# Two token tiles first: reordering attention's output projection, with two plain units instead of three in the FFN behind it

## The chip, the cores and the metric

The kernel runs on one core of a Trainium2 chip. The metric is device time in microseconds, here the median of several executions. Engines are named as in the profile: PE (matmuls), PEld (PE's weight loads), DVE (vector engine), ACT (scalar engine), POOL and SP (which here mostly issue transfers).

## The reference

A trunk of two layers over 512 tokens of width 1024, all in float32. Layer 0 mixes tokens by stick-breaking attention with 16 heads, layer 1 by a gated token MLP; each is followed by a SwiGLU FFN of width 2816. The part that matters is attention's output projection, the residual step, and the first FFN:

```python
y = o.transpose(0, 2, 1, 3).reshape(B, S, D) @ w_o          # attention's projection
x = x + gate * rms_norm(y, mix_post_g[i])
shift, scale, gate = ada_modulation(c, ffn_ada_w[i], ffn_ada_b[i])
h = rms_norm(x, ffn_pre_g[i]) * (1.0 + scale) + shift
y = (jax.nn.silu(h @ w_gate) * (h @ w_up)) @ w_down
x = x + gate * rms_norm(y, ffn_post_g[i])
```

## The kernel before, in words

**Numbers in two parts.** Every matmul operand is split into a rounded high part and a low part (`split`, line 128), and every product is three matmuls, high by high, high by low and low by high (`mm3`, line 120). ACT writes the high part and DVE the low part. Weights are loaded raw into two buffers (`wraw`) and split into a pair of tiles `wh` and `wl`. These come from `wpool` with five slots, to which `wpool2` with one is added after attention; `wtile` (line 184) takes them in turn from the pools that exist when it is called. A slot is free again when the last matmul that reads it is done.

**The stream of weights.** `stream` is one list of all weights in the order of use. `wget(key, look)` hands out the next one and splits those up to `look` places ahead (3 unless said otherwise) where that hasn't been done.

**Attention and filler.** Eight head pairs are worked on in an order written out by hand. Between their steps a generator, `filler`, puts in other matmuls, a group of three at a time: first the q and k of later pairs (112 groups), then the beginning of the output projection for token tiles 3 and 2 (16 groups: `NEARLY` = 4 of the 8 weight slabs, two tiles, two halves of 512 columns). `FIRST`, `FILLS` and `LAST` say how many groups go into each place.

**The projection (`out_proj`).** There are four tiles of 128 tokens, each with two PSUM banks, which is all eight banks. The first slabs go through all tiles (tiles 2 and 3 have slabs 0 to 3 already); the last `J` = 4 slabs are kept and applied tile by tile in the order 0, 1, 2, 3, so that the tiles finish one after another. After each comes `boundary`: squares on ACT, scaling, the residual sum and the second norm on DVE, a store of x by POOL's queue, eight transposes on PE, and the split of the transposed result (`hTh`, `hTl`). Tiles 0 and 1 are the lower 256 tokens, tiles 2 and 3 the upper. From attention's end on, the order within an engine is the scheduler's, which goes by program order and by what is ready, within the dependencies (several matmuls into one bank keep their order).

**The first FFN.** Its 2816 hidden columns are 22 units of 128. A plain unit (`Ffn.unit`) multiplies gate and up separately, and can do 256 tokens alone. A seven-product unit (`seven`) makes both by seven products of sums of weights with sums of the transposed halves, S1 to S4. Its weights are built by `blocks` from `rawx` and `rawy` (three `wh`/`wl` pairs and one smaller). The sums combine a lower tile with its upper one: `boundary` keeps a copy `c` of the lower tiles, and `sums` makes S1 to S4 when the upper ones are there. Now there are three plain units (`NH` = 3) and 19 seven-product units. The lower halves of the three plain units run among the boundaries of tiles 2 and 3, the upper halves after them, then the seven-product units begin. The weights that `wget` emits in the second of them stand in the program inside the last boundary (`mid`).

The FFN's products are in this order, each over four k:

```python
product(R1, "A11", "B11", True, False)
product(R2, "A12", "B21", True, True)
product(R3, "1", "T1", True, False)
product(R1, "2", "T2", False, False)
product(R3, "4", "B22", False, True)
product(R1, "3", "T3", False, False)
product(R1, "A22", "T4", False, True)   # in rest(), inside the next unit
```

Of the kernel before, what the change touches and what calls it, by code (L numbers as in the profile page):

```python
# [33 lines left out]
def trunk(ctx: ExitStack, tc: tile.TileContext, A: dict, out: bass.AP):  # L34
# [273 lines left out]
        ap = A[key]  # L308
        stream.append((ap[idx], a, b, (key,) + idx))

    NH = 3
    wadd("wv", 2, 512, 0, 0)
    wadd("wqk", 8, P, 0, 0)
    wadd("wqk", 8, P, 0, 1)
# [7 lines left out]
    for k in range(KD):  # L322
        wadd("wo", 1, D, k)
    for l in range(2):
        for f in range(NH):
            wadd("wgu", 8, P, l, f, 0)
            wadd("wgu", 8, P, l, f, 1)
        for f in range(NH, KF):
            stream.append((None, 0, 0, ("blocks", (l, f - NH))))
        if l == 1:  # L330
            for q in range(2):
                for p in PAIRS[q]:
                    wadd("wdn", 4, 256, q, p)
        if l == 0:
            for f in range(KF):
                wadd("wdown", 1, D, f)
            for j in range(4):
# [152 lines left out]
        lo %= 256  # L490
        return h[:, k % 4, lo : lo + n], l[:, k % 4, lo : lo + n]

    def boundary(s, tt, y, xin, hT, S, tag, mid=None):
# [12 lines left out]
        xd[tt] = dram.tile([P, D], F32, tag=f"x{tt}", bufs=2, name=nm("xd"))  # L506
        nc.gpsimd.dma_start(out=xd[tt][:], in_=x)
        sx = small.tile([P, 1], F32, tag="sx", name=nm("sx"))
        feature[1] = act.activation(junk[:], x[:], AF.Square, accum_out=sx[:])
        sd, r1 = rms(sx[:])  # L510
        dve.tensor_tensor(t[:], x[:], ada["A", s], ALU.mult)
        dve.reciprocal(r1[:], sd[:])
        feature[0] = dve.scalar_tensor_tensor(
            t[:], t[:], r1[:, 0:1], ada["B", s], ALU.mult, ALU.add
        )
        late = []
        if mid is not None:
            mid()
            chain = pe["prev"]
        for q in range(2):  # L520
            ps = bank("tp", tag)
            for k in range(4):
                kk = q * 4 + k
                transpose(ps[:, k * P : (k + 1) * P], t[:, kk * P : (kk + 1) * P])
                if mid is not None and kk == 0:
                    order(last_tp[0], chain)
            a = ps[:].rearrange("p (a b) -> p a b", a=4)
            if tt % 2 == 0:
                hT[tt // 2, q] = (slot(F32R, "hTh", 4, 256), slot(F32R, "hTl", 4, 256))
            c = slice(tt % 2 * P, (tt % 2 + 1) * P)  # L530
            th, tl = hT[tt // 2, q]
            split(th[:, :, c], tl[:, :, c], a)
            if S is not None and tt < 2:
                if tt == 0:
                    S["c", q] = slot(F32, "c", 4, 256)
                act.activation(S["c", q][:, :, tt * P : (tt + 1) * P], a, AF.Copy)
            late.append(a)
        return lambda: sums(S, tt, late)

    def sums(S, tt, a):  # L540

# [27 lines left out]
        return t  # L569


    def out_proj(s, nk, get_act, wkey, J, bg, hT, nxt=(), pre=None, S=None, steps=0, bg2=None):

# [6 lines left out]

        def step(k, tt, a, w, halves=(0, 1)):
            for hf in halves:
                if k == 0 or k == mid and tt == last:
                    y[tt][hf] = bank("y", "p" if tt == last else "b")
                mm3(
                    y[tt][hf][:],
                    a[0][:, tt * P : (tt + 1) * P], a[1][:, tt * P : (tt + 1) * P],
                    w[0][:, 0, hf * 512 : (hf + 1) * 512],  # L590
                    w[1][:, 0, hf * 512 : (hf + 1) * 512],
                    k == 0 or k == mid and tt == last, k == nk - 1 or k + 1 == mid and tt == last,
                )

        npre = 0
        if pre is not None:
            npre = len(pre["w"])
            for tt in pre["y"]:
                y[tt] = pre["y"][tt]
        for k in range(nk - J):  # L600
            a = get_act(k)
            w = pre["w"][k] if k < npre else wget(wkey(k))
            for tt in range(NT):
                if k >= npre or tt not in pre["y"]:
                    step(k, tt, a, w)
# [10 lines left out]
            (k, get_act(k), wget(wkey(k), J + 1 if k == nk - J else 0))  # L616
            for k in range(nk - J, nk)
        ]
        sqrt_table()
        xs = {tt: x_load(tt) for tt in range(2)}  # L620
        xin = xs.get
        for tt in range(NT):
            for hf in range(2):
                for k, a, w in tail:
                    step(k, tt, a, w, (hf,))
            if tt == last and yp is not None:
                for hf in range(2):
                    dve.tensor_tensor(yp[:, hf, :], y[tt][hf][:], yp[:, hf, :], ALU.add)
                y[tt] = [yp[:, hf, :] for hf in range(2)]
            if tt < 2:  # L630
                boundary(s, tt, y[tt], xin, hT, S, "p" if last == 0 else "b")
                xs[tt + 2] = x_load(tt + 2)
        evacs, late = [], []
        for n, tt in enumerate((2, 3)):
# [5 lines left out]
            if nxt and tt == 2:  # L640
                evacs.append(nxt[0]())
            late.append(
                boundary(
                    s, tt, y[tt], xin, hT, S, "p" if tt == 3 else "b",
                    mid if nxt and tt == 3 else None,
                )
            )
        if nxt:
            evacs.append(nxt[2]())
            with tc.issue_after(last_sqrt[0].ins):  # L650
                for f in evacs:
                    f()
# [204 lines left out]
    with tc.tile_pool(name="att", bufs=1) as att, tc.tile_pool(name="att2", bufs=2) as att2:  # L857
# [282 lines left out]
    fwork["pool"] = fpool  # L1140

    class Ffn:
        def __init__(self, s, li, hT, S):
            self.s, self.li, self.hT, self.S = s, li, hT, S
            self.act = []
            self.ws = {}

        def w(self, f, look):
            if f not in self.ws:
# [22 lines left out]
            return evac  # L1172

        def first(self):
            return [lambda f=f: self.unit(f, 0, 256, 2) for f in range(NH)]

        def seven(self, f, pending, bg0):

            W = wget(("blocks", (self.li, f - NH)), 0)
# [52 lines left out]
            return rest  # L1232

        def units(self, bg0):
            for f in range(NH):
                self.unit(f, 256, 256)()
            rest = None
            for f in range(NH, KF):
                if f == NH:
                    act.chain = True  # L1240
                if f == NH + 1:
# [215 lines left out]
    def gmlp(bg, hT, nhT, nS, nxt):  # L1457
# [120 lines left out]
def _layout(i):  # L1578
# [31 lines left out]
    a["wx"], a["wy"] = [np.stack(t) for t in zip(*[blocks(g[3:], u[3:]) for g, u in gu])]  # L1610
# [66 lines left out]
```

## Time and profile before

| | |
|---|---|
| device time, median of 3 runs | 1106.31 us (1104.22 to 1106.82) |
| span of the profiled execution | 1104.6 us, 18512 instructions |
| PE busy | 1085.9 us (98%) |
| DVE busy | 945.9 us (86%) |
| ACT busy | 594.2 us (54%) |
| first matmul of the projection outside attention | about 243.4 us |
| first seven-product unit of the first FFN begins | 312.5 us |

No time of the profiled execution is given besides its span, from its first to its last instruction; the span lies between the lowest and the highest of the three times. A busy PE is not a PE at its peak, because matmuls overlap: a matmul of 512 columns is shown with some 390 ns, while one starts every 227 ns. So the cost of matmuls is read from the chain of waits, where a stretch of them is given with its length and count. In the rows, `y` is the projection's output, `tp` the transposes, `gu` a plain unit's gate and up, `r` the banks of a seven-product unit, `raw` a loaded weight, `fs` and `Sl` the sums.

### The profile page before, as it was taken

What the parts mean: (1) busy time and instruction counts of PE and PEld (TensorE: products, weight loads), DVE (VectorE), ACT (ScalarE), POOL (GpSimd) and SP (SyncE); (2) the same over time, 40 slices, a digit from 0 to 9 for tenths busy, and PEclk for the clock granted to TensorE, in tenths of its full rate; (3) what the DMA queues carried; (4) which work ended last, traced back from release to release, by engine and by line L of the source; (5) the groups of instructions that cost most, each with busy time, mean ns of one, the idle gap of its engine ahead of it and who ended that gap; (6) DMA issues with size and microseconds to landing.
All of it is one profiled execution on the core that took longest, in us unless ns stands there. A gap on an engine that the chain in (4) does not pass through costs nothing.

```text
span 1104.6 us, 18512 instructions
## 1 busy us (share of the span) xinstructions
PE 1085.9 (98%) x7404; PEld 979.0 (89%) x7404; DVE 945.9 (86%) x1248; ACT 594.2 (54%) x982; POOL 29.5 (3%) x53
## 2 busy tenths in 40 slices
PE   6999999999999999999999999999999999999997
PEld 4787788788999999998888889988999999989996
DVE  4988999966989999989866967668979999899997
ACT  6554665665655555554243626426555555565662
POOL 0020100000000000000000000001000000000000
PEclk9999999999999999999999999999999999999999
DMA  8976434304433434359757465334334343333252
GB/s 302 370 226 217 142 116 133 125 11 152 157 112 131 162 119 146 132 197 351 272 191 256 144 205 196 96 116 155 128 117 155 128 159 102 110 115 96 77 187 81
DMA packets 51355, 176.38 MB, mean 160 GB/s; under 512 B 6074, under 2 KB 9146, under 8 KB 51268
## 3 DMA queue, kind: packets, MB, share of 16 engines
q1 hardware_dynamic: 48708, 166.81, 44.6%
q0 software_dynamic: 2560, 8.39, 2.1%
q8 instruction: 58, 0.95, 0.3%
q14 instruction: 29, 0.24, 0.1%
HBM read 164.69 MB, written 8.39 MB: 157 GB/s over the span
## 4 chain that ended last, share of the span: by engine, by line
PE 90%; DVE 4%; DMA 2%; ACT 2%; issue 1%; SPq 0%; DVEq 0%; ACTq 0%
PE r L109 32%; PE y L109 18%; PE pqk L109 7%; PE gu L109 6%; PE v L109 5%; PE X L109 4%; PE u L109 4%; PE Y L109 3%; PE av L109 2%; PE z L109 2%; PE tw L117 1%; PE tp L117 1%; PE Z L109 1%; PE W L109 1%; PE ab L109 1%
## 5 line engine op out<-in xcount | busy, mean ns | idle before, releaser
L87 ACT ACTIVATE wh<-raw 128x1024 fp32r<-128x1024 f32 (+1 forms) x112 | 115.7, 1038 | 130.5 <-PE y L109 39.4
L109 PE MATMUL r<-Sh,wh 128*128 128x256 f32 x608 | 168.1, 276 | 0.5 <-ACT e L87 0.5
L109 PE MATMUL r<-Sh,wl 128*128 128x256 f32 x608 | 167.9, 276 | 0.0
L109 PE MATMUL r<-Sl,wh 128*128 128x256 f32 x608 | 167.9, 276 | 0.0
L109 PE MATMUL y<-wh,as 128*128 128x512 f32 x480 | 149.9, 390 | 0.0
L178 DVE TENSOR_TENSOR wl<-raw,wh 128x1024 fp32r<-128x1024 f32 x87 | 105.8, 1222 | 48.2 <-ACT wh L87 47.6
L109 PEld LDWEIGHTS r<-Sh,wh 128*128 128x128 f32 x608 | 114.1, 188 | 1.0 <-ACT e L87 0.9
L109 PEld LDWEIGHTS r<-Sl,wh 128*128 128x128 f32 x608 | 114.1, 188 | 0.1
L109 PEld LDWEIGHTS r<-Sh,wl 128*128 128x128 f32 x608 | 114.1, 188 | 0.0
L109 PEld LDWEIGHTS y<-wh,as 128*128 128x128 f32 x480 | 90.0, 188 | 18.6
L71 DVE TENSOR_TENSOR wl<-f,wh 128x1024 fp32r<-128x1024 f32 x87 | 103.2, 1220 | 0.0
L87 ACT ACTIVATE wh<-f 128x1024 fp32r<-128x1024 f32 x87 | 91.8, 1055 | 15.3 <-DVE f L71 11.6
L87 ACT ACTIVATE e<-r 128x256 f32<-128x256 f32 x114 | 43.7, 385 | 101.8 <-PE r L109 100.8
L109 PE MATMUL y<-wl,as 128*128 128x512 f32 x240 | 93.7, 391 | 0.0
L109 PE MATMUL r<-hTh,wh 128*128 128x256 f32 x304 | 84.2, 277 | 0.2 <-DVE gu L71 0.2
L109 PE MATMUL r<-hTl,wh 128*128 128x256 f32 x304 | 84.0, 276 | 0.0
L109 PE MATMUL r<-hTh,wl 128*128 128x256 f32 x304 | 84.0, 276 | 0.0
L109 PE MATMUL r<-hTh,b 128*128 128x256 f32 x304 | 57.9, 276 | 0.0
L109 PEld LDWEIGHTS r<-hTh,wh 128*128 128x128 f32 x304 | 57.1, 188 | 0.9 <-DVE gu L71 0.9
L109 PEld LDWEIGHTS r<-hTh,wl 128*128 128x128 f32 x304 | 57.1, 188 | 0.0
L109 PEld LDWEIGHTS r<-hTl,wh 128*128 128x128 f32 x304 | 57.1, 188 | 0.0
L87 ACT ACTIVATE wh<-rawx 128x1024 fp32r<-128x1024 f32 x38 | 40.4, 1063 | 29.8 <-PE r L109 29.0
(262 smaller groups left out, 2937.1 us busy)
## 6 DMA issues: line engine op xcount, KB each, us to landing
rawada<-in_ada SPq DMA_DIRECT2D x80, 512.0 KB, 5.7
rawy<-in_wy SPq DMA_DIRECT2D x38, 512.0 KB, 4.6
rawx<-in_wx SPq DMA_DIRECT2D x38, 512.0 KB, 3.7
raw<-in_wdown SPq DMA_DIRECT2D x22, 512.0 KB, 5.4
raw<-in_wdn SPq DMA_DIRECT2D x22, 512.0 KB, 3.6
raw<-in_wqk SPq DMA_DIRECT2D x16, 512.0 KB, 3.9
ada<-in_ada0p SPq DMA_DIRECT2D x12, 512.0 KB, 6.3
raw<-in_wgu SPq DMA_DIRECT2D x12, 512.0 KB, 3.5
```

Source lines behind the costliest of these rows:

```text
L71: b = getattr(nc.vector, op)(*args, **kw)
L87: b = nc.scalar.activation(*args, **kw)
L109: b = nc.tensor.matmul(o, l, r, start=start, stop=stop, skip_group_check=True)
L117: last_tp[0] = nc.tensor.transpose(o, i, ident)
L178: last_low[0] = nc.vector.tensor_tensor(l[:], raw[:], h[:].bitcast(F32), ALU.subtract)
```

## The change

1. `NH` is 2 for the first FFN and 3 for the second. The first FFN has two plain units and 20 seven-product units. The arrays `wx` and `wy` hold one block more.
2. `NEARLY` is 5: slab 4 of the projection is applied to tiles 3 and 2 in attention too, so the filler has 20 groups there. `LAST` has four groups more, one in head pair 6 and three in head pair 7.
3. With `up=True`, slabs 0 to 3 are not applied to tiles 0 and 1 at the projection's beginning. Those tiles start with slab 4. `J` is 2. The tiles finish in the order 2, 3, 0, 1; tiles 0 and 1 take slabs 6 and 7 and then slabs 0 to 3 (`early`).
4. `boundary` keeps the copy `c` of the upper tiles, and `sums_up` makes S1 at once from their two halves; S2, S4 and S3 follow after tiles 0 and 1.
5. The plain units do the upper 256 tokens first, among the boundaries of tiles 0 and 1, and the lower ones after.

```diff
-    NH = 3
+    NH = 2, 3
...
-        for f in range(NH, KF):
-            stream.append((None, 0, 0, ("blocks", (l, f - NH))))
+        for f in range(NH[l], KF):
+            stream.append((None, 0, 0, ("blocks", (l, f - 2))))
...
-            if S is not None and tt < 2:
-                if tt == 0:
+            if S is not None and tt in lead:
+                if tt % 2 == 0:
                     S["c", q] = slot(F32, "c", 4, 256)
-                act.activation(S["c", q][:, :, tt * P : (tt + 1) * P], a, AF.Copy)
+                act.activation(S["c", q][:, :, c], a, AF.Copy)
             late.append(a)
-        return lambda: sums(S, tt, late)
+        if lead == (0, 1):
+            return lambda: sums(S, tt, late)
+        return lambda: sums_up(S, tt, late)
+
+    def sums_up(S, tt, a):
...
+        if tt > 1:
+            dve.tensor_tensor(f[:, 0], c0, c1, ALU.subtract)
+            part("1", f[:, 0])
+            return
+        g = npool.tile([P, 2, 4, P], F32, tag="n", name=nm("fs"))
+        dve.tensor_tensor(f[:, 0], a[0], c0, ALU.subtract)
+        dve.scalar_tensor_tensor(f[:, 1], f[:, 0], -1.0, c1, ALU.mult, ALU.subtract)
+        part("2", f[:, 1])
+        dve.tensor_tensor(g[:, 1], f[:, 1], a[1], ALU.add)
+        part("4", g[:, 1])
+        part("3", f[:, 0])
...
-        for k in range(nk - J):
+        for k in range(npre - 1 if up else 0, nk - J):
...
+        early = [(k, get_act(k), pre["w"][k]) for k in range(npre - 1)] if up else []
         sqrt_table()
-        xs = {tt: x_load(tt) for tt in range(2)}
+        seq = (2, 3, 0, 1) if up else (0, 1, 2, 3)
+        xs = {tt: x_load(tt) for tt in seq[:2]}
         xin = xs.get
-        for tt in range(NT):
+        for n, tt in enumerate(seq):
             for hf in range(2):
-                for k, a, w in tail:
+                for k, a, w in tail + (early if n > 1 else []):
                     step(k, tt, a, w, (hf,))
...
-            evacs.append(nxt[2]())
+            evacs.extend(f() for f in nxt[2:])
...
-        NEARLY = 4
+        NEARLY = 5
...
-        LAST = (2, 2, 2, 2, 2, 2, 1), (1, 1, 1, 1, 1, 1, 1), (2, 0, 2, 0, 2, 2, 0)
+        LAST = (2, 2, 2, 2, 2, 2, 1), (2, 1, 1, 1, 1, 1, 1), (3, 1, 2, 1, 2, 2, 0)
...
-            return [lambda f=f: self.unit(f, 0, 256, 2) for f in range(NH)]
+            return [lambda f=f: self.unit(f, self.lo, 256, 2) for f in range(self.nh)]
...
-    f0, f1 = Ffn(1, 0, hT1, S1), Ffn(3, 1, hT3, S3)
+    f0, f1 = Ffn(1, 0, hT1, S1, 256), Ffn(3, 1, hT3, S3, 0)
     out_proj(
         0, KD, lambda k: (o8[k][:, 0, :], o8[k][:, 1, :]), lambda k: ("wo", k),
-        4, bg, hT1, f0.first(), early, S1,
+        2, bg, hT1, f0.first(), early, S1, up=True,
     )
```

More of the change, by code (lines that the diff above doesn't have):

```diff
@@ L324, in trunk @@
     for l in range(2):
-        for f in range(NH):
+        for f in range(NH[l]):
             wadd("wgu", 8, P, l, f, 0)
             wadd("wgu", 8, P, l, f, 1)
-        for f in range(NH, KF):
-            stream.append((None, 0, 0, ("blocks", (l, f - NH))))
+        for f in range(NH[l], KF):
+            stream.append((None, 0, 0, ("blocks", (l, f - 2))))
         if l == 1:
@@ L491, in hB, with boundary @@
         return h[:, k % 4, lo : lo + n], l[:, k % 4, lo : lo + n]
-    def boundary(s, tt, y, xin, hT, S, tag, mid=None):
+    def boundary(s, tt, y, xin, hT, S, tag, mid=None, lead=(0, 1)):
         halves = [slice(0, 512), slice(512, D)]
@@ L532, in boundary, with part @@
             split(th[:, :, c], tl[:, :, c], a)
-            if S is not None and tt < 2:
-                if tt == 0:
+            if S is not None and tt in lead:
+                if tt % 2 == 0:
                     S["c", q] = slot(F32, "c", 4, 256)
-                act.activation(S["c", q][:, :, tt * P : (tt + 1) * P], a, AF.Copy)
+                act.activation(S["c", q][:, :, c], a, AF.Copy)
             late.append(a)
-        return lambda: sums(S, tt, late)
+        if lead == (0, 1):
+            return lambda: sums(S, tt, late)
+        return lambda: sums_up(S, tt, late)
+    def sums_up(S, tt, a):
+        c = slice(tt % 2 * P, (tt % 2 + 1) * P)
+        if tt % 2 == 0:
+            for n in "1" if tt == 2 else "324":
+                S[n] = (slot(F32R, "Sh", 4, 256), slot(F32R, "Sl", 4, 256))
+        c0, c1 = [S["c", q][:, :, c] for q in range(2)]
+        f = npool.tile([P, 2, 4, P], F32, tag="n", name=nm("fs"))
+        def part(n, f):
+            split(S[n][0][:, :, c], S[n][1][:, :, c], f)
+        if tt > 1:
[9 more added lines that the diff above has]
+        part("3", f[:, 0])
     def sums(S, tt, a):
@@ L569, in x_load, with out_proj @@
         return t
-    def out_proj(s, nk, get_act, wkey, J, bg, hT, nxt=(), pre=None, S=None, steps=0, bg2=None):
+    def out_proj(s, nk, get_act, wkey, J, bg, hT, nxt=(), pre=None, S=None, steps=0, bg2=None, up=False):
         last = 0 if steps else 3
@@ L584, in step @@
             for hf in halves:
-                if k == 0 or k == mid and tt == last:
+                if k == (npre - 1 if up else 0) or k == mid and tt == last:
                     y[tt][hf] = bank("y", "p" if tt == last else "b")
@@ L591, in step @@
                     w[1][:, 0, hf * 512 : (hf + 1) * 512],
-                    k == 0 or k == mid and tt == last, k == nk - 1 or k + 1 == mid and tt == last,
+                    k == (npre - 1 if up and tt < 2 else 0) or k == mid and tt == last,
+                    k == (npre - 2 if up and tt < 2 else nk - 1) or k + 1 == mid and tt == last,
                 )
@@ L629, in out_proj @@
                 y[tt] = [yp[:, hf, :] for hf in range(2)]
-            if tt < 2:
-                boundary(s, tt, y[tt], xin, hT, S, "p" if last == 0 else "b")
-                xs[tt + 2] = x_load(tt + 2)
+            if n < 2:
+                f = boundary(
+                    s, tt, y[tt], xin, hT, S, "p" if tt == last else "p" if last == 0 else "b",
+                    None, seq[:2],
+                )
+                xs[seq[n + 2]] = x_load(seq[n + 2])
+                if up:
+                    f()
         evacs, late = [], []
-        for n, tt in enumerate((2, 3)):
+        for n, tt in enumerate(seq[2:]):
             def mid():
@@ L638, in mid @@
                 edge[0] = False
-            if nxt and tt == 2:
+            if nxt and n == 0:
                 evacs.append(nxt[0]())
@@ L644, in out_proj @@
                     s, tt, y[tt], xin, hT, S, "p" if tt == 3 else "b",
-                    mid if nxt and tt == 3 else None,
+                    mid if nxt and n == 1 else None, seq[:2],
                 )
@@ L1142, in trunk, with __init__ @@
     class Ffn:
-        def __init__(self, s, li, hT, S):
-            self.s, self.li, self.hT, self.S = s, li, hT, S
+        def __init__(self, s, li, hT, S, lo):
+            self.s, self.li, self.hT, self.S, self.lo = s, li, hT, S, lo
             self.act = []
             self.ws = {}
+            self.nh = NH[li]
         def w(self, f, look):
@@ L1174, in first @@
         def first(self):
-            return [lambda f=f: self.unit(f, 0, 256, 2) for f in range(NH)]
+            return [lambda f=f: self.unit(f, self.lo, 256, 2) for f in range(self.nh)]
         def seven(self, f, pending, bg0):
-            W = wget(("blocks", (self.li, f - NH)), 0)
+            W = wget(("blocks", (self.li, f - 2)), 0)
             prep = ahead()
@@ L1234, in units @@
         def units(self, bg0):
-            for f in range(NH):
-                self.unit(f, 256, 256)()
+            for f in range(self.nh):
+                self.unit(f, 256 - self.lo, 256)()
             rest = None
-            for f in range(NH, KF):
-                if f == NH:
+            for f in range(self.nh, KF):
+                if f == self.nh:
                     act.chain = True
-                if f == NH + 1:
+                if f == self.nh + 1:
                     pe["chain"] = dve.chain = act.chain = True
@@ L1609, in _layout @@
     a["wgu"] = np.stack([np.stack([g[:3], u[:3]], 1) for g, u in gu])
-    a["wx"], a["wy"] = [np.stack(t) for t in zip(*[blocks(g[3:], u[3:]) for g, u in gu])]
+    a["wx"], a["wy"] = [np.stack(t) for t in zip(*[blocks(g[2:], u[2:]) for g, u in gu])]
     a["wdown"] = slabs(i["ffn_w_down"][0])
```

## The prediction, made before the change was run

> **What bounds the kernel now.** I read the page first, then the stretches around the change, the chain of waits, and last the timelines of ACT and DVE in those stretches.
>
> ```profile
> span 1104.6 us, 18512 instructions
> PE 1085.9 (98%) x7404; PEld 979.0 (89%) x7404; DVE 945.9 (86%) x1248; ACT 594.2 (54%) x982; POOL 29.5 (3%) x53
> PE 90%; DVE 4%; DMA 2%; ACT 2%; issue 1%; SPq 0%; DVEq 0%; ACTq 0%
> ```
>
> PE is the bound nearly everywhere, so a change gains only matmuls that vanish or PE idle time that is filled. By stretch (time, then busy time of PE, PEld, DVE, ACT, POOL):
>
> ```profile
> 229.00:243.40 14.40, 13.98 (x88) 11.77 (x85) 7.93 (x11) 7.97 (x13) 0.00 (x0) 1.00 0.01 1
> 243.40:257.70 14.30, 14.30 (x65) 11.83 (x64) 8.18 (x9) 7.34 (x11) 0.00 (x0) 1.00 0.38 111
> 257.70:316.90 59.20, 58.84 (x434) 54.70 (x432) 55.00 (x79) 36.24 (x70) 3.12 (x5) 1.00 0.46 152
> 317.10:494.00 176.90, 176.90 (x1553) 176.72 (x1554) 159.41 (x209) 99.51 (x169) 0.96 (x1) 1.00 0.40 139
> ```
>
> These are the last head pair of attention, the start of its projection, the passage into the first FFN, and that FFN's seven-product units. In the passage PE is full, but DVE is busy 55.0 of 59.2: a second bound close behind. The chain and PE's waits there:
>
> ```profile
> 243.42 22.23 PE y L109 x98
> ...
> 277.46 5.71 PE gu L109 x48
> 283.18 0.87 PE tp L117 x8
> 284.05 5.50 PE gu L109 x48
> 289.55 1.08 PE tp L117 x8
> 290.63 21.88 PE gu L109 x192
> 312.51 4.09 PE r L109 x36
> ...
> 316.65 0.39 ACT e L87
> ...
> 317.09 163.78 PE r L109 x1440
> ...
> PE av L109 <- DVE ar L71: 0.8, 1, 0.8
> PE r L109 <- ACT e L87: 0.5, 1, 0.5
> PE av L109 <- ACT ar L87: 0.4, 1, 0.4
> ```
>
> A projection matmul costs 22.23/98 = 0.227 us, an FFN matmul 163.78/1440 = 0.1137 us. All PE idle that the change could fill is 0.8 + 0.4 + 0.5 = 1.7 us.
>
> **The change, part by part.**
>
> *Two plain units instead of three.* A plain unit has 2 x 2 x 8 x 3 = 96 matmuls, a seven-product unit 7 x 4 x 3 = 84. 12 x 0.1137 = -1.4 us. The extra unit's preparation lies beside PE: in its stretch ACT is busy 99.5 and DVE 159.4 of 176.9. Two weight loads go and two of the same size come.
>
> *Four projection steps moved into the last two head pairs.* 12 matmuls x 0.227 = 2.7 us move; they gain only where PE waits there, so 0 to -1.2. I take -0.4, the last pair's gap, since the added steps stand right ahead of that wait.
>
> *The weight slots.* This decides it. The rounded weights live in five slots of `wpool`; the sixth, `wpool2`, joins only after attention. `wget` rounds three slabs ahead, so with `NEARLY` = 5 all eight projection slabs are assigned to the five. Slabs 0 to 3 are now read by the last matmuls of tiles 0 and 1, so four slots stay taken to the end of the projection, and slabs 4, 5, 6 and 7 pass one after another through the fifth. Within a bank the accumulation keeps its order, so slabs 0 to 3 cannot go first. Rows of ACT (start, duration, what ended its idle time) and one of DVE show what a slot that comes free costs:
>
> ```profile
> 246.19 1.07 ACT L87 ACTIVATE wh<-raw 128x1024 fp32r<-128x1024 f32 x1 [0.28 <-PE y L109]
> 248.91 1.06 ACT L87 ACTIVATE wh<-raw 128x1024 fp32r<-128x1024 f32 x1 [1.65 <-PE y L109]
> 252.27 1.06 ACT L87 ACTIVATE wh<-raw 128x1024 fp32r<-128x1024 f32 x1 [2.30 <-DMA raw<-in_wo]
> ...
> 247.29 1.23 DVE L178 TENSOR_TENSOR wl<-raw,wh 128x1024 fp32r<-128x1024 f32 x1 [0.33 <-ACT wh L87]
> ```
>
> The first two are slabs 5 and 6 waiting for slabs 0 and 1. Today PE has other slabs meanwhile; after the change it has none. It stands from its last matmul to the end of ACT's rounding: 1.07 plus about 0.25 for the matmul's tail and the two signals, 1.3 us. DVE's low part (1.23) is covered by the first product of the eight banks, 8 x 0.227 = 1.8. Three hand-overs: +3.9 us; from 0 (if another slot is found) to 3 x 2.6 = 7.8 (if the low part isn't covered). Slab 7's load is issued when slab 5's rounding frees its raw buffer, some 9 us before it is due, so SP adds nothing. Behind ACT's waiting rounding stand only the squares of tiles not yet finished.
>
> *Reordered tail.* Matmuls and transposes (4 x 8) are the same in number. But slab 7 starts only when all tiles have had slab 6, so tiles 2 and 3 finish together and late. From 243.4: +2.7 - 0.4 of moved work = 245.7; slab 4 for two tiles 2.7; then stall 1.3 and slab 5 5.4, the same for slab 6, and stall 1.3: 263.2. Tile 2 ends some 2 us later and its first multiplication on DVE starts at 265.5. Tile 0's starts now at
>
> ```profile
> 257.79 0.69 DVE L71 TENSOR_TENSOR t<-y,G 128x512 f32<-128x512 f32 x1 [0.70 <-ACT junk L87]
> ...
> 313.45 1.29 DVE L71 TENSOR_TENSOR Sl<-fs,Sh 128x512 fp32r<-128x512 f32 x2
> ...
> 314.98 1.22 DVE L71 TENSOR_TENSOR wl<-f,wh 128x1024 fp32r<-128x1024 f32 x1
> ```
>
> and the passage's DVE work ends at 314.98 + 1.22 = 316.2, the last sum at 314.7. DVE's groups in that stretch (count, then busy and mean ns):
>
> ```profile
> L178 DVE TENSOR_TENSOR wl<-raw,wh 128x1024 fp32r<-128x1024 f32 x5 | 5.9, 1220 | 0.0
> L71 DVE TENSOR_TENSOR hTl<-tp,hTh 128x512 fp32r<-128x512 f32 x8 | 5.3, 686 | 0.4
> L71 DVE TENSOR_TENSOR Sl<-fs,Sh 128x512 fp32r<-128x512 f32 x8 | 5.3, 686 | 0.1
> L71 DVE TENSOR_TENSOR wl<-f,wh 128x1024 fp32r<-128x1024 f32 x4 | 4.9, 1220 | 0.0
> L71 DVE TENSOR_TENSOR f<-rawx,rawy 128x1024 f32<-128x1024 f32 x2 | 2.5, 1225 | 0.6 <-DMA rawx<-in_wx 0.6
> L71 DVE TENSOR_TENSOR wl<-rawx,wh 128x1024 fp32r<-128x1024 f32 x2 | 2.4, 1224 | 0.3 <-ACT wh L87 0.3
> L71 DVE TENSOR_TENSOR act<-silu,gu 128x256 f32<-128x256 f32 x6 | 2.3, 414 | 0.0
> ```
>
> *S1 at the upper boundaries.* Sixteen operations for the sums before and after (eight combinations, eight low parts): 0. Only their order changes; S1 was never what is late.
>
> *Less cover.* After the change DVE loses one rounding in this stretch (four of four instead of five of six, 1.2) and two `act` products (0.8): 53.0 us of work. Starting at 265.5 it ends at 318.5 without any idle time, at 322.5 with today's share of it (59.2/55.0). PE, if DVE never made it wait, would come to the first seven-product unit at 245.7 + 132 x 0.227 + 32 transposes (4.3) + 4 x 48 x 0.1137 (21.8) + 3.9 = 305.7. (The same sum for today gives 243.4 + 32.7 + 4.3 + 32.7 = 313.1; the chain says 312.5.) S3 is needed five products (6.8 us) later, and the last sum stands 1.5 ahead of the end of DVE's work. So the unit can start at 310.2 to 314.2, which is 4.5 to 8.5 late; if the second block of weights is put behind the sums (1.2 + 1.4 + 3.6 = 6.2 of this work) nearly nothing to 2.3 late. Bounds 0 and +8.5. I take +4.9, in the middle of what the order can give, since no row shows that order.
>
> *The rest.* The four stores on POOL's queue and the four loads of x on SP's are the same, in tile order 2, 3, 0, 1; each has over 10 us. Tile 1's transposes now use the six common PSUM banks: two gate/up banks and four of transposes fill them, so the lower units wait for the upper ones' silu. That is 0 to +2 (a table load and two small steps), inside DVE's lag, so 0.
>
> *Sum.* Against today's 312.5 + 0.5: 305.7 + one more unit of 84 x 0.1137 (9.55) = 315.2, so +2.2 with PE's stalls alone, and with DVE's lag 4.9, +7.1. What follows shifts by as much. The profiled span is 1104.6, 0.4 over the lowest of the three times and 1.7 under their median of 1106.31. Median: 1106.3 + 7.1 = 1113.4.
>
> **The rivals.** *PE's stalls alone:* the scheduler puts the second block behind the sums and DVE is never late: +2.2, 1108.5. For it: the first unit needs only the first block. Against: DVE was busy 93% of the passage when it began 8 us earlier. It decides if the first S group finds S1 to S4 finished.
> *No stall, the other side:* the slots don't bind. Place: ACT's three roundings after attention; price -3.9 and the lag, which leaves -1.4 - 0.4 - 0.5 = -2.3, 1104.0 (at most -3.1). For it: the manual order is off here, so the scheduler may move things. Against: the slot count and the in-bank order. It decides if a slab's rounding starts before the last matmul on the slab before it.
> *The second block first:* both blocks are emitted inside tile 1's boundary, ahead of its transposes. The lag reaches 8.5 and the last tile's evacuation, no longer covered by a third unit, adds about 2 (half the transposes 0.5, a rounding on ACT and the low part on DVE of 0.7 each): +12.7, 1119.0.
>
> *The clock falls.* A lag taken in one piece could idle PE for 4 us or more. The only such gap now is at the start, in the waits and stretches:
>
> ```profile
> PE tp L117 <- DVE x L71: 8.7, 2, 7.8
> ...
> 4.00:8.00 4.00, 0.16 (x1) 0.16 (x2) 1.13 (x5) 1.44 (x3) 0.00 (x0) 1.00 0.93 306
> 8.00:12.00 4.00, 3.16 (x15) 2.76 (x16) 2.15 (x6) 3.84 (x9) 0.00 (x0) 1.00 1.02 416
> ```
>
> After 7.8 us of idle PE the granted clock is still 1.00. If a gap here halved it for as long as a gap of 4 us, 4 us of matmuls would take 4 us more: +11, 1117.5. [...]
>
> **How the numbers follow.** Chances: the forecast 0.55 (its own range +3.5 to +11), stalls alone 0.20, no stall 0.12, the second block first 0.10, the clock 0.03. This kernel's three times spread by 0.24%, so 0.3% (3.3 us) is about what can be told from no change. Slower: 0.55 + 0.10 + 0.03 and a small part of the stalls alone, 0.72. Faster needs more than the no-stall case's -3.1, so 0.05 from causes that I don't see. Same: 0.23. The range reaches from 1105.0, which leaves out most of the no-stall case, to 1119.0.
>
> **What would show it.** After: ACT's roundings of slabs 5, 6, 7 each end a PE wait of about 1.3 us between 248 and 264; DVE's first t at about 265; the seven-product stage begins near 311, and has 20 units. Wrong, if PE runs through the projection without waits, or if DVE has idle time while PE enters the seven-product stage.

## The result, and the profile after

The changed kernel takes 1122.75 us (median of 5 runs, 1120.76 to 1124.85), the kernel before 1106.31 (5 runs). The ratio is 1.0153, with a 95% interval of 1.0140 to 1.0165: slower by 16 us, and outside the predicted range of 1105.0 to 1119.0. From the page of the changed kernel, the span and the busy times:

```profile
span 1121.0 us, 18501 instructions
PE 1089.1 (97%) x7392; PEld 980.8 (87%) x7392; DVE 950.7 (85%) x1255; ACT 596.9 (53%) x987; POOL 29.5 (3%) x53
PE 86%; DVE 7%; DMA 3%; ACT 2%; issue 1%; SPq 0%; DVEq 0%; ACTq 0%
```

No engine has more work worth speaking of, but 7% of the chain that ended last is now DVE's (4% before). PE's waits from 235 to 345 us, the passage (engine, tile and line, what was waited for: us in all, times, longest):

```profile
PE tp L117 <- DVE t L71: 4.0, 1, 4.0
PE y L109 <- ACT wh L87: 3.4, 3, 1.1
PE tp L117 <- DVE ss L71: 2.9, 1, 2.9
PE gu L109 <- DVE hTl L71: 2.5, 2, 1.7
PE gu L109 <- ACT hTh L87: 1.2, 2, 1.0
```

That is 14 us, where the kernel before has one wait of 0.5 in the same stretch (for `e`). The y line is the slabs. The other four all wait for a tile's boundary. Where DVE lost its time is seen by stretches (length, then busy us of PE, PEld, DVE, ACT and POOL, then the granted clock). Of the kernel before:

```profile
256.00:270.00 14.00, 13.97 (x66) 11.39 (x65) 10.79 (x17) 7.13 (x17) 1.09 (x2) 1.00 0.53 184
270.00:290.00 20.00, 19.98 (x144) 18.35 (x144) 19.46 (x28) 16.07 (x33) 2.03 (x3) 1.00 0.45 158
```

and of the changed kernel:

```profile
256.00:270.00 14.00, 12.85 (x57) 10.31 (x56) 6.28 (x10) 4.90 (x12) 0.55 (x1) 1.00 0.51 177
270.00:290.00 20.00, 14.18 (x68) 11.41 (x67) 14.75 (x22) 12.49 (x24) 0.54 (x1) 0.87 0.36 117
290.00:310.00 20.00, 15.14 (x108) 14.54 (x107) 19.79 (x28) 10.96 (x21) 2.02 (x3) 0.88 0.29 104
```

At 290 us DVE has done 4.5 us less work in the first stretch (10.79 - 6.28) and 4.7 less in the second (19.46 - 14.75), 9.2 in all. From there to 310 it is full (19.79 of 20) while PE stands a quarter of the time.

The first loss is the late start. ACT's roundings of slabs 5, 6 and 7, and DVE's first operation of a boundary:

```profile
247.16 1.06 ACT L87 ACTIVATE wh<-raw 128x1024 fp32r<-128x1024 f32 x1 [0.32 <-PE y L109]
254.04 1.06 ACT L87 ACTIVATE wh<-raw 128x1024 fp32r<-128x1024 f32 x1 [5.83 <-PE y L109]
260.93 1.06 ACT L87 ACTIVATE wh<-raw 128x1024 fp32r<-128x1024 f32 x1 [5.83 <-PE y L109]
...
264.91 0.69 DVE L71 TENSOR_TENSOR t<-y,G 128x512 f32<-128x512 f32 x1 [1.67 <-ACT junk L87]
```

The second loss is a waiting line that the prediction did not see. DVE's rows at the second and third boundary of the order, tiles 3 and 0:

```profile
271.17 0.16 DVE L71 RECIPROCAL r<-sd 128x1 f32<-128x1 f32 x1 [0.42 <-ACT sd L87]
...
273.90 0.69 DVE L71 TENSOR_TENSOR hTl<-tp,hTh 128x512 fp32r<-128x512 f32 x1 [1.15 <-ACT hTh L87]
275.26 0.69 DVE L71 TENSOR_TENSOR fs<-c,c 128x512 f32<-128x512 f32 x1 [0.67 <-ACT c L87]
275.87 1.28 DVE L71 TENSOR_TENSOR t<-y,G 128x512 f32<-128x512 f32 x2
...
289.66 0.69 DVE L71 TENSOR_TENSOR fs<-c,c 128x512 f32<-128x512 f32 x1 [0.66 <-ACT c L87]
290.27 1.28 DVE L71 TENSOR_TENSOR t<-y,G 128x512 f32<-128x512 f32 x2
```

Tile 3's norm factor r is there at 271.3, so its `y` has long been squared; yet its first multiplication t starts at 275.87, right behind `fs`, the scratch of S1, of tile 2. The same again at 289.66 and 290.27 for tile 0. `t` and `fs` come from one pool of two buffers, `npool` (lines 497 and 549), and the program asks for them in this order: t of tile 2, fs of tile 2, t of tile 3, fs of tile 3, t of tile 0. So tile 2 alone takes both buffers, and t of tile 3 has none until tile 2 has given one back; in the trace it comes only behind fs of tile 2, which waits for tile 2's transposes and its copies `c`. In the kernel before the sums are made after the last boundary, and two tiles' t overlap. So far this is an argument from the program; the experiment with the scratch below tests it. The last boundary in DVE's rows, and some pieces of the chain that ended last (start, us, what):

```profile
303.94 2.35 DVE L71 TENSOR_TENSOR f<-rawx,rawy 128x1024 f32<-128x1024 f32 x2
...
308.55 1.29 DVE L71 TENSOR_TENSOR hTl<-tp,hTh 128x512 fp32r<-128x512 f32 x2
```

```profile
278.86 1.23 DVE wl L178
...
280.11 4.15 DMA raw<-in_wgu
...
286.69 3.40 DMA rawx<-in_wx
...
309.30 11.06 PE gu L109 x95
320.35 9.75 PE r L109 x86
```

The lower units wait for tile 1's `hTl`, at 308.6, and the seven-product units begin at 320.35 (312.51 before, with one unit less to come). That is 7.8 + 9.55 = 17.4 us of delay; less PE's wait of 0.5 for `e`, which has gone, 16.9, close to the 16.4 by which the spans differ.

### The profile page after: what moved, and what is told of

It is laid out like the page before. It is cut to its first block, busy times and chain, and to the rows that moved or that the text cites. A ratio compares the mean times of both kernels' runs of the same rounds, so it can differ in the third digit from the quotient of the medians.

```text
span 1121.0 us, 18501 instructions
## 1 busy us (share of the span) xinstructions
PE 1089.1 (97%) x7392; PEld 980.8 (87%) x7392; DVE 950.7 (85%) x1255; ACT 596.9 (53%) x987; POOL 29.5 (3%) x53
## 4 chain that ended last, share of the span: by engine, by line
PE 86%; DVE 7%; DMA 3%; ACT 2%; issue 1%; SPq 0%; DVEq 0%; ACTq 0%
PE r L109 32%; PE y L109 16%; PE pqk L109 7%; PE v L109 5%; PE X L109 4%; PE gu L109 4%; PE u L109 4%; PE Y L109 3%; PE av L109 2%; PE z L109 2%; PE tw L117 1%; PE Z L109 1%; PE W L109 1%; PE tp L117 1%; PE ab L109 1%
## 5 line engine op out<-in xcount | busy, mean ns | idle before, releaser
L87 ACT ACTIVATE wh<-raw 128x1024 fp32r<-128x1024 f32 (+1 forms) x110 | 113.4, 1036 | 137.8 <-PE y L109 49.0
L109 PE MATMUL r<-Sh,wh 128*128 128x256 f32 x624 | 172.3, 276 | 0.0
L109 PE MATMUL r<-Sh,wl 128*128 128x256 f32 x624 | 172.2, 276 | 0.0
L109 PE MATMUL r<-Sl,wh 128*128 128x256 f32 x624 | 172.2, 276 | 0.0
L178 DVE TENSOR_TENSOR wl<-raw,wh 128x1024 fp32r<-128x1024 f32 x85 | 103.4, 1221 | 55.0 <-ACT wh L87 54.4
L109 PEld LDWEIGHTS r<-Sh,wh 128*128 128x128 f32 x624 | 117.1, 188 | 0.2 <-ACT e L87 0.2
L109 PEld LDWEIGHTS r<-Sl,wh 128*128 128x128 f32 x624 | 117.1, 188 | 0.1
L109 PEld LDWEIGHTS r<-Sh,wl 128*128 128x128 f32 x624 | 117.1, 188 | 0.0
L71 DVE TENSOR_TENSOR wl<-f,wh 128x1024 fp32r<-128x1024 f32 x89 | 105.5, 1220 | 0.7 <-ACT wh L87 0.7
```

The lines of the kernel that those rows point to most:

```text
L71: b = getattr(nc.vector, op)(*args, **kw)
L87: b = nc.scalar.activation(*args, **kw)
L109: b = nc.tensor.matmul(o, l, r, start=start, stop=stop, skip_group_check=True)
L178: last_low[0] = nc.vector.tensor_tensor(l[:], raw[:], h[:].bitcast(F32), ALU.subtract)
```

## The experiments

Each time below is a median beside runs of the kernel before on the same chip (1106.05, 1106.52, 1105.61 and 1106.41 in the four groups); "+" is what the ratio makes of 1106.

**The two parts alone.** Two plain units with the old order, and the new order with three:

```diff
 e4_two_units:   NH = 2, 3; the projection as before (NEARLY = 4, up=False, lower tokens first)
 e8_three_units: the changed kernel with NH = 3, 3
```

> Two plain units instead of three alone; projection, boundaries and sums in the order of the kernel before (tiles 0, 1, 2, 3, four slabs kept, S1 to S4 after tiles 2 and 3). The count of matmuls gives -1.4 us. A: DVE's work of the passage is nearly the same (54 us) while PE has 10.9 us less to do beside it, and DVE had 4 to 5 us in hand, so PE stands for 4 to 7 us: +3 to +6 against the kernel before, 1109 to 1112. If the lost cover cost nothing: 1105.

> The changed order (tiles 2 and 3 first, slabs 0 to 3 kept, S1 early) with three plain units as before. With a third unit the blocks are emitted behind the last boundary and PE has 10.9 us more to do beside it. A: the slot waits and the boundaries one behind the other stay, so that the order alone costs most: +8 to +11 against the kernel before, 1114 to 1117. Rival (all is the lost cover, and the order hardly matters): +3.4 for the slot waits only, 1109.5.

The two units took 1111.23 (ratio 1.0049, 1.0034 to 1.0064), +5.4, within what theory A of that run expected (+3 to +6). The order alone took 1121.41 (1.0142, 1.0127 to 1.0157), +15.7, more than either theory of its run had. Together they cost 1.0153, less than the sum. PE's longest waits in the first, then in the second:

```profile
PE gu L109 <- DVE hTl L71: 3.4, 1, 3.4
PE r L109 <- ACT e L87: 0.6, 1, 0.6
```

```profile
PE tp L117 <- DVE t L71: 6.8, 3, 4.0
PE y L109 <- ACT wh L87: 3.4, 3, 1.1
```

So the third plain unit was cover for the last boundary: without it PE waits 3.4 us for `hTl`, even in the old order. And the order brings the slab stalls and the late t whatever the number of units.

**Scratch and slots.** The two suspected buffers, each by itself and both:

```diff
 e1_scratch
-        f = npool.tile([P, 2, 4, P], F32, tag="n", name=nm("fs"))
+        if tt > 1:
+            f = fpool.tile([P, 2, 4, P], F32, tag="f13", name=nm("fs"))
+        else:
+            f = npool.tile([P, 2, 4, P], F32, tag="n", name=nm("fs"))
 e2_slots: slabs 5 and 7 in wpool2, slab 6 in a slot of wpool; in attention wget looks
           no further than slab 4
+            wpools[1][0] if key in (("wo", 5), ("wo", 7)) else wpool if key == ("wo", 6) else None
 e3_both: e1_scratch and e2_slots
```

> Theory A (two causes): besides the three hand-overs of the one weight slot, the boundaries run one behind the other because S1's scratch tile is taken from npool, whose two slots are handed out in program order: tile 3's first multiplication (t) stood until tile 2's scratch had its slot, at 275.9 us, and tile 0's until tile 3's, at 290.3. Here that scratch comes from another pool. A expects the three waits of about 1.15 us on ACT's rounding as they are, tile 3's t at about 270 instead of 275.9, DVE's idle time between 265 and 290 (6 us) mostly gone, and 5 to 7 us less than the changed kernel: about 1116. Rival B (the late start and DVE's amount of work alone): the scratch doesn't matter, the order of DVE stays as it is, within 1 us of the changed kernel's 1122.7.

> Slabs 5 and 7 take the sixth slot and slab 6 the fifth; the scratch stays in npool. A: the three waits on ACT's rounding (3.4 us) go, tile 2 finishes some 6 us earlier (it no longer has to wait until all tiles have had slab 6), and all that follows moves up with it, but the boundaries stay one behind the other: 5 to 7 us less than the changed kernel, about 1116.5. B: the late start is the whole cause, so that moving it up by 6 to 7 us gives the passage back its cover: 12 us or more less, about 1109. Rival C (the slot waits cost only themselves): 3.4 us less, 1119.3.

> Both edits: a sixth slot for the slabs and the scratch outside npool. A: 11 to 14 us less than the changed kernel, 1109 to 1112, and what is left over the kernel before is the cover lost with the third plain unit. If nothing else were at work, it would be the gain first counted, 1104. B and C: the same as with the slots alone.

| kernel | time | ratio | PE waits for slabs | first t |
|---|---|---|---|---|
| changed kernel | 1122.75 | 1.0153 (1.0140 to 1.0165) | 3.4 | 264.91 |
| scratch | 1118.28 | 1.0105 (1.0088 to 1.0122) | 3.4 | 264.68 |
| slots | 1114.41 | 1.0074 (1.0059 to 1.0089) | none | 255.06 |
| both | 1112.99 | 1.0058 (1.0039 to 1.0076) | none | 257.33 |

Both are real: the scratch is worth some 5 us, the slots some 8 to 9, together about 10, so they overlap. With the scratch elsewhere, t of tile 3 starts at 270.36 instead of 275.87, and DVE is full from 270 to 290, where it had been idle for 5 us:

```profile
270.36 0.68 DVE L71 TENSOR_TENSOR t<-y,G 128x512 f32<-128x512 f32 x1
```

```profile
270.00:290.00 20.00, 16.30 (x102) 13.77 (x100) 19.71 (x30) 14.82 (x31) 1.07 (x2) 1.00 0.39 135
```

So the shared pool did hold the boundaries apart. The slots give more than the 3.4 us of PE's waits. Counted from the first matmul on slab 4 (244.35, 244.16, 242.82 and 245.11 in the table's order), the first t comes after 20.5 us with the stalls and after 12.2 without, 8.3 us sooner: in the chain of the kernel with the slots 49 matmuls stand from there to tile 2's end, in that of the changed kernel 68 and the three stalls. DVE, which is late from there on, gets that time. Against the expectations, the scratch gave a little less than theory A's 5 to 7 us, the slots more (between A's 1116.5 and B's 1109), and both together ended 1 us above A's 1109 to 1112. They still leave +6, with PE's waits

```profile
PE gu L109 <- DVE hTl L71: 3.7, 1, 3.7
PE tp L117 <- DVE t L71: 2.2, 1, 2.2
```

**Three units with both mended.** If scratch and slots are all that the order costs, then with the third unit nothing should be left.

```diff
 e9_three_healed: e3_both with NH = 3, 3
```

> The new order with three plain units, S1's scratch in a pool of its own and the last slabs of the projection in slots of their own; the blocks of the sixth feature tile as in the changed kernel. Three units with the order alone took 1121.41. Theory A (scratch and slots are all that the order costs): the 6.8 us of waiting for t and the 3.4 for the slabs go, and with them the slow clock; the time comes back to that of the kernel before, 1104 to 1108. Rival B (a last boundary behind a longer tail of the projection costs by itself, whatever the scratch does): 1110 to 1115, with a wait of 3 us or more left before the last transposes.

1108.36 (1.0016, 1.0005 to 1.0027), +1.8, just above theory A's 1104 to 1108 and below rival B's 1110. So of the order's +15.7 some 14 are the two buffers. What PE still waits for in the passage is one line:

```profile
PE tp L117 <- DVE t L71: 1.8, 1, 1.8
```

and the chain reaches the seven-product units at 312.29 (312.51 before):

```profile
290.43 21.86 PE gu L109 x192
312.29 22.78 PE r L109 x201
```

In this execution PE had waited 7.5 us for `x` at the start of the kernel, in most others about 9, so the passage stands 1.5 to 2 us early here; by the median the order is not quite free. Its twelve executions lie in two groups, 1104.0 to 1105.8 at a mean clock of 0.999 and 1107.7 to 1109.6 at 0.997 to 0.998. From this kernel to the one with two units (1.0058) it is some 4.6 us: the lost cover again, as in the old order.

**The blocks of the first seven-product units** (an expectation calls them the blocks of the sixth feature tile). In the changed kernel DVE works on the first seven-product units' weights (`f`, `wl`) ahead of tile 1's `hTl`. Three kernels emit that work behind the last boundary, and two more also hold the first block's roundings and low parts behind it by dependencies.

```diff
 e5_blocks (from the changed kernel), e7_two_units_blocks (from e4), e6_all (from e3)
-            return [lambda f=f: self.unit(f, self.lo, 256, 2) for f in range(self.nh)]
+            def ready():
+                while len(got) < taken[0] + 2:
+                    wemit()
+                return lambda: None
+            return [lambda: self.unit(0, self.lo, 256, 2), lambda: self.unit(1, self.lo, 256, 0), ready]
 e10_late (from e6): also
+            if len(got) == first_blocks[0]:
+                order(b, feature[0])
 e11_late_three: the same dependencies in e9
```

> The changed kernel with one edit: the first two blocks of seven-product weights are emitted behind the last boundary (as in the kernel before) and not inside it. Theory D: the second of two plain units looks as far ahead as the second of three did and so pulls both blocks into the last boundary, ahead of its transposes; DVE then does 4.6 us of block work (304.0 to 308.6) between tile 1's h and its hTl, on which PE stands. D expects tile 1's hTl to start some 3 to 4.5 us earlier, PE's wait for hTl (2.5 us in all) to become under 1, and 2.5 to 4.5 us less: 1118 to 1120. Rival: the block work is only moved behind, DVE's amount decides, and PE waits the same time later for the sums: within 1 us of 1122.7.

> Two units alone (order of the kernel before) with the blocks behind the last boundary. D: the 3.4 us wait for hTl there goes, 1111.2 falls to about 1108; the cover that is really lost is then 2 us or so. Rival (the cover itself): the waits move behind to the sums, within 1 us of 1111.2.

> Sixth slot, scratch outside npool, and the blocks behind the last boundary, together. If the three causes are all there is, what is left is DVE's amount of work against PE's shorter cover: PE's waits of 5.9 us with the first two edits fall by 2.5 to 4, and the time to 1109 or 1110. The rival (DVE's amount decides) expects the 1113.0 measured without the blocks.

> The version with two units, scratch, slots and blocks behind (1109.59), and the first block's roundings and low parts besides held behind the last boundary. There the x block's low part and its wait, 1.87 us, stand on DVE between the last tile's x and its t, and PE waits 2.9 us for that t. Theory C (the last gap and the slow clock that follows it are what is left): t comes 1.9 us sooner, the gap is about 1 us, the units behind it take 10.9 to 11.2 us instead of 12.99, and the seven-product stage starts at 304.5 to 306 instead of 307.9: 1105.8 to 1107.5. Rival D (DVE's work only moves): PE waits for the sums or the block in the first seven-product unit instead, 2 to 3 us, and the time stays at 1108.5 to 1110.

> The same holding back of the first block, with three units, scratch and slots. Theory A with C: 1104 to 1107, level with the kernel before or up to 0.2% faster. Rival B: above 1109, the same as three units without the holding back.

In the changed kernel it gains nothing (1122.67, where theory D had 1118 to 1120), in the old order with two units it loses about 3 (1114.00, ratio 1.0076 against 1.0049), where neither theory had a loss, and with both buffers mended it gains about 3 (1109.59, 1.0032, 1.0019 to 1.0046), as expected. Holding back the first block as well loses 5 (1114.87, 1.0079, 1.0064 to 1.0093), which neither theory had; with three units it changes nothing (1106.58, 1.0015, against 1.0016), within theory A's 1104 to 1107. So the place of the blocks does not explain the changed kernel's loss, and moving them helps only when the two buffers are mended. A wait in the old order with the blocks behind, and PE's longest in the kernel with the first block held back:

```profile
PE r L109 <- ACT Sh L87: 3.4, 1, 3.4
```

```profile
PE gu L109 <- DVE act L71: 3.2, 1, 3.2
```

In the first the wait moved from `hTl` to the sums; in the second to a small `act` product, which in DVE's rows had come behind the blocks, at 305.69, and which holds the bank of the next plain unit. In these two kernels, whatever was put first, something else ended last; that with two units there isn't time for all of it under PE is the likely reason, but no run tests it by itself.

**The clock.** In several of these traces PE's pauses are followed by a lower granted clock. In the changed kernel, the transposes behind its longest pause, and the stretches after it:

```profile
283.80 1.15 PE L117 MATMUL tp<-identt,t 128*128 128x128 f32 x8 [4.02 <-DVE t L71]
```

```profile
285.00:290.00 5.00, 3.27 (x13) 2.97 (x14) 3.90 (x5) 3.51 (x6) 0.00 (x0) 0.50 0.43 129
...
300.00:305.00 5.00, 5.00 (x39) 5.00 (x38) 5.00 (x7) 3.30 (x6) 1.49 (x2) 0.82 0.25 105
```

To tell what this costs, three kernels put transposes of the identity, which nothing uses, into pauses; the bank is overwritten by what follows.

```diff
 e12_filled (from e6): 10 ahead of tile 1's transposes; e13_three_filled (from e9): 8
+                for _ in range(10):
+                    transpose(ps[:, :P], ident)
+                    order(last_tp[0], chain)
+                    chain = last_tp[0]
 e14_after_filled (from the changed kernel): 16 ahead of the first upper unit's matmuls,
           11 ahead of tile 0's transposes
```

> The version with two units, scratch, slots and blocks behind (1109.59), with ten transposes of the identity into the bank that the last tile's transposes overwrite, ahead of these: they fill about 2.4 of the 2.9 us in which PE waits for t, and compute nothing that is used. Theory C (the clock falls because PE stood idle, and the slow units behind are on the path): the clock stays at 0.95 or more from 290 to 300, the plain unit's matmuls take 10.9 to 11.3 us instead of 12.99, and the time falls by 1.5 to 2.2 us, to 1107.4 to 1108.1. Rival E (the clock falls there for another reason, or DVE's work is as late as the units): within 0.5 of 1109.6.

> The new order with three units, scratch and slots (1108.36, in two groups of runs: 1104.0 to 1105.8 and 1107.7 to 1109.6), with eight transposes of the identity that nothing uses ahead of the last tile's, where PE waits 1.8 us for t. Theory C (the upper group is the clock that falls behind this pause in some executions): all runs fall into the lower group, median 1104 to 1106, no more than 0.1% from the kernel before. Rival E (the two groups have another cause): both groups stay, median 1107 to 1109.

> The changed kernel (1122.75) with PE's pauses of 4.0 and 2.9 us, ahead of the third and the fourth tile's transposes of that order, filled with sixteen and eleven transposes of the identity that nothing uses. Theory C with DVE as the bound (the slow clock there is hidden, since PE waits for DVE's hTl afterwards): the clock stays at 0.95 or more from 285 to 305, yet the time is within 1.5 of 1122.7. Rival F (the slow units delay the boundaries themselves, through the roundings that wait for the transposes or the banks that come free late): 1117 to 1120.5.

The two stretches behind the pause of 2.9 us in the kernel with scratch, slots and blocks mended, and the lower plain units in its chain, and then the same rows with the pause filled:

```profile
290.00:295.00 5.00, 2.49 (x10) 1.97 (x10) 5.00 (x8) 2.61 (x6) 0.00 (x0) 0.69 0.00 0
295.00:300.00 5.00, 5.00 (x28) 5.00 (x29) 4.63 (x8) 1.57 (x3) 0.00 (x0) 0.62 0.47 129
```

```profile
294.89 12.99 PE gu L109 x95
```

```profile
290.00:295.00 5.00, 2.55 (x19) 1.88 (x17) 5.00 (x8) 3.57 (x7) 0.00 (x0) 1.00 0.14 60
295.00:300.00 5.00, 4.95 (x43) 4.95 (x44) 5.00 (x9) 1.66 (x3) 0.00 (x0) 1.00 0.46 136
```

```profile
295.05 11.06 PE gu L109 x95
```

DVE's work in the two is in the same order. With the pause filled the clock stays at 1.00, and the same 95 matmuls take 11.06 us instead of 12.99: the pause is the cause of the slow clock, which is worth 1.9 us there. That is theory C's half. In the time nothing is seen of it: 1109.14 (1.0032, 1.0020 to 1.0044) against 1109.59 with the same ratio, within the 0.5 us that rival E expected. Of its six executions three show a clock of 0.996 over the span, three 0.999, so the filling, which leaves two pauses of 1.1 us, seems to have kept the clock up only in some; but the times of the two kinds overlap. Filling the three-unit kernel gives 1107.06 (1.0005, 0.9996 to 1.0014), level with the kernel before, at a clock of 0.998 or more in all eleven executions; theory C had 1104 to 1106. But they still spread from 1104.95 to 1108.01, so the two groups seen with three units aren't the clock alone.

In the changed kernel the filling gained nothing: 1124.63 (1.0167, 1.0153 to 1.0181), where theory C had no change and rival F 1117 to 1120.5. The sixteen took only 1.9 us, so the first pause was cut to 2.3 and the clock still fell, to 0.65 from 285 to 290. The second pause was filled:

```profile
300.00:305.00 5.00, 4.90 (x44) 4.66 (x42) 5.00 (x8) 3.50 (x8) 1.37 (x2) 1.00 0.26 105
```

```profile
308.91 0.39 PE L109 MATMUL gu<-hTl,wh 128*128 128x256 f32 x1 [3.38 <-DVE hTl L71]
```

There PE runs at 1.00 instead of 0.82, and waits 3.38 us for tile 1's `hTl` instead of 1.7. A faster PE only waits longer: in the changed kernel the slow clock of that stretch costs nothing that can be seen beside DVE. And the longer wait has its own slow clock behind it: 0.66 from 310 to 315, where the 95 matmuls of the lower units take 12.73 us instead of 11.06. So the time of this run can't settle what the slow clock costs the changed kernel, and for the first stretch nothing is shown.

## Why the prediction was wrong

The direction was right, and two steps held almost to the number. *The weight slots*: three hand-overs of 1.15 us (ACT's rounding of 1.06 and 0.09; the 0.25 was the author's estimate, which no row shows), 3.4 for 3.9 predicted. *Reordered tail*: the first t at 264.9 for 265.5, in part by luck: slab 4 begins at 244.35, not at 245.7, because the four moved steps cost less than their -0.4 allowed (PE's two waits for `ar` in attention are gone), and from there to the first t it is 20.6 us, not 19.8. DVE's work, 53.0 us predicted, is 52.7 from 264.9 to the end of the sums at 324.2. The rest of what would show it did not come: the seven-product units began at 320.35, not near 311.

- *S1 at the upper boundaries*, put at 0 ("Only their order changes; S1 was never what is late"), is the step that failed. S1 itself is in time, but its scratch stands in the pool of t, and makes the boundaries of tiles 2, 3 and 0 run one behind the other. Taking it out gives back about 5 us by itself: 1118.28 instead of 1122.75. The prediction had counted the operations and their cover and not asked which buffers they take.
- *Less cover*: a lag of 4.9 (0 to 8.5) was taken from DVE's work at its present density (55.0 of 59.2, 93%). But DVE was idle for over 5 us of the 20 from 270 to 290, because the boundaries waited for each other (0.3 with the scratch elsewhere). The lag was 320.35 - 305.7 = 14.6, beyond its bound: this is the second step that failed. Some 5 of the 9.7 us above the forecast of 4.9 are the scratch; the rest, of which the lost cover below is a likely part, was not taken apart. Nor was the late item the sums, which it argued from: PE waited for tile 1's boundary, and the sums of the first unit came in time.
- *Two plain units instead of three*: -1.4 counts the matmuls rightly, but by itself this part costs +5.4. The third unit's first half stood over the last boundary; its loss was named as a +2 in one rival, and the sum has no term for it.
- *The weight slots* were right as stalls of PE, yet mending them is worth 8 to 9 us: they hold back DVE's start by 8.3, and DVE is what ends last. The prediction had that start, but took for its price the middle of the lag's range.
- *The clock falls*, with a chance of 0.03, came true as a behaviour: a gap of 4.02 us and then 0.50. It had been weighed by one long gap at the start of the kernel, where the granted clock reads 1.00. That row was misread: the transposes behind that gap run at half their later pace (0.246 and 0.123 us), as the last section shows. Its price of +4 (with the 7.1 that is 1117.4, where the prediction has 1117.5) took a clock halved for as long as the gap, which no row of the kernel before shows; in the changed kernel the clock read 0.50 from 285 to 290 and 0.85 from 290 to 295. The price was not what made the difference, as far as the filled pauses show.
- The prediction also left out that the third `wgu` load, from 280.11 to 284.26, and the block's load, from 286.69 to 290.09, stand in the chain; the first starts when DVE has finished with a raw buffer (`wl`, 278.86 and 1.23).

None of the versions beats the kernel before; the best is the new order with three units, both buffers mended and the pause filled (1.0005).

## What to carry to other kernels

When an operation is moved between two others, list the buffers it takes and who else takes them in program order: a scratch tile in a pool of two can put stages one behind the other that used to overlap, without any operation getting longer. When work that covers a late engine is taken away, cost it by what that engine still has to do before its result is needed, not by the matmuls saved. And a stall is worth more than its own length when another engine that is late anyway starts only behind it: here 3.4 us of stalls were worth 8 to 9.

## What the runs showed of the hardware

In these traces the granted clock fell after pauses of PE in the middle of a kernel: to 0.50 from 285 to 290 us after 4.02 us in the changed kernel, to 0.69 and 0.62 from 290 to 300 after 2.9 in the kernel with scratch, slots and blocks mended. The stalls of 1.15 us at the changed kernel's slabs, 5.8 us apart, left it at 1.00 from 246 to 270. After pauses just under 2 us it went both ways: behind the one of 1.84 us in the three-unit kernel with both buffers mended it stayed at 1.00 in the profiled execution, and behind one of 1.86 us in the same kernel with the first block held back it fell to 0.72. There eight transposes take 1.91 us, where the other execution has 1.09:

```profile
292.05 1.91 PE L117 MATMUL tp<-identt,t 128*128 128x128 f32 x8 [1.86 <-DVE t L71]
```

```profile
290.00:295.00 5.00, 3.14 (x16) 2.95 (x15) 4.45 (x6) 4.98 (x9) 0.07 (x1) 0.72 0.35 111
```

So in these traces the length of the pause alone doesn't decide.

The start of the kernel before, on which the prediction rested, belongs here too. The column of the granted clock shows 1.00 there, but the chain of waits has transposes of one kind twice, 8 soon after the pause of 7.8 us and 11 some 8 us later:

```profile
10.65 1.97 PE tp L117 x8
...
18.89 1.35 PE tp L117 x11
```

That is 0.246 us for each and then 0.123. PE went at half its later pace there, so the column doesn't tell the pace at the start of this kernel. Whether the pause is the reason, or every kernel starts so, no run here separates.
